# The order of the products with the high and the low part of the weights inside one unit of a panel

## The chip, the cores and the metric

The kernel runs on one core of one Trainium2 chip. The metric is the time of one execution on the device in microseconds (us); of the kernel before there are three runs, and their median counts. One more execution was recorded by the profiler; all rows of the trace come from that one.

## The reference

A decoder trunk of two layers over 256 tokens with a model width of 2048, in 32-bit floats. What matters here is that nearly all of its work is products of a matrix of activations (256 tokens x 2048) with matrices of weights:

```
z = h @ w_in                                   # layer 0: gated linear attention, layer 1: forgetting attention
x = x + concatenate([o, m]) @ w_out            # o: the mixer's heads, m: four heads that attend to 256 memory tokens
u = causal_dwconv(h @ w_up, conv_w, conv_b)    # the channel mixer, 2048 -> 2 x 5632, depthwise convolution of width 3
a, val = split_cols(u, [FFN_HIDDEN, FFN_HIDDEN])
x = x + (silu(a) * val) @ w_down               # 5632 -> 2048
```

h is x after an RMS norm. Between the two layers keys, values and forget gates of the second layer are computed from x in the same way.

## The kernel before, in words

**Two parts of each number.** TensorE multiplies numbers of the type fp32r. Each activation and each weight is split into a high part, rounded to that type, and a low part, the rest. A product is then three products: high with high, high with low and low with high. An activation chunk is a tile `[128, 2, 256]` (bufA and bufB, sixteen each): 128 features on the partitions, then the high part of 256 tokens and behind it the low part.

**Panels and units.** The weights are repacked on the host into panels (`_panels`, `_layout`), in the order of use. A panel's weights come in units of up to 1024 columns of 128 rows, 512 KB, and each unit has one load. There are two kinds of panels:

- 122 panels with *features on the partitions* (`fm`, multiplied by `proj_fm`, L213): 256 output features, 16 chunks of 128 input features, four units of four chunks. They make the keys, queries and gates, and the up-projection of both channel mixers (88 of the 122).
- 42 panels with *tokens on the partitions* (`tm`, `proj_tm`, L248): values, the output projections and the down-projections. There the activations are the stationary operand, and each chunk has three products, high x high at L272, the weights' low part at L273, and the activations' low part at L274. In a panel 512 columns wide each of them has 512 moving columns. The change doesn't touch them.

**A unit of proj_fm.** `split_unit` (L204) loads a unit (`raw`, four buffers, queue of SyncE, L198 and L200), casts it to the high part on ScalarE (`whi`, three buffers, L201), and subtracts on VectorE for the low part (`wlo`, three buffers, L210). Then for each of its four chunks j and each half c of the 256 output features `product` (L232) is called. The weights are the stationary operand, 128x128, loaded into TensorE for each product. With the high part of the weights the moving operand is the whole chunk, 512 columns (the high part of the tokens, then their low part, L235); with the low part it is the chunk's high part alone, 256 columns (L236). Both add to the accumulator of c, a PSUM tile of 512 columns (`acc`, four buffers, two to a panel). So a unit has eight products with the high part and eight with the low part, taken in turn. In a panel's last chunk the low part comes first, and the high part ends the accumulation (L238).

**After a panel.** `evac` of each half: ScalarE copies the second 256 columns out (`whole`, L243), VectorE adds the first 256 (L245), and what follows depends on the panel. In the channel mixer that is the convolution, the activation, and the split of the result into the next chunk (L306, L310).

**What sets the order.** The code's order is a wish: a planner simulates the engines and gives each of them a fixed list of instructions. It takes them by priority, which is the place in the code, and where one isn't ready by its own estimates of time it takes a later one first. Instructions on one accumulator keep their order. `tc.high_priority(offset=AHEAD)` around `split_unit` pulls loads, casts and subtractions 300 places ahead. On the chip each engine works off its list in order and waits on semaphores.

**Start of a stage.** The sixteen chunks for a panel come from the stage before: transposes of the stream on TensorE (L842), then the split into two parts on ScalarE and VectorE (L309, L310). Chunks 12 to 15 come last.

Of the kernel before, what the change touches and what calls it, by code (L numbers as in the profile page):

```python
# [19 lines left out]
P = 128  # L20
T = 256
# [117 lines left out]
def _trunk(ctx: ExitStack, tc: tile.TileContext, xt, xtok, memt, wp, wgu, gns, gfin, cnv, par, msk, out):  # L139
    nc = tc.nc  # L140
    where, _ = _layout()
    V, S, TE = nc.vector, nc.scalar, nc.tensor
# [8 lines left out]
    part = const.tile([P, C_N], F32, name="part")  # L151
# [52 lines left out]
    def split_unit(unit, pieces=1, before=None, pool=wpool, whole=False):  # L204
        with tc.high_priority(offset=AHEAD):
            raw, hi, w = load_unit(unit, pieces, before, pool, whole)
            lo = pool.tile([P, NUNIT], F32R, name="wlo", tag="wlo", bufs=3)
            for i in range(pieces):
                s = slice(i * w // pieces, (i + 1) * w // pieces)
                V.tensor_tensor(lo[:, s], raw[:, s], hi[:, s].bitcast(F32), ALU.subtract)  # L210
        return hi, lo

    def proj_fm(key, src, evac, before=None):  # L213

        units = where[key]
        total = sum(len(u[1]) for u in units)
        acc = [pacc.tile([P, 512], F32, name="acc", tag="acc") for _ in range(2)]
        base = min(min(u[1]) for u in units)
        done = 0
        for n, unit in enumerate(units):  # L220
            if before is None:
                hi, lo = split_unit(unit)
            else:
                hi, lo = split_unit(unit, 2, lambda half: before(n, half), whole=n > 0)
            for j, kc in enumerate(unit[1]):
                for c in range(2):
                    product(acc[c], c, total - 1, done, src[kc - base], hi, lo, j)
                done += 1
        for c in range(2):
            evac(c, acc[c])  # L230

    def product(a, c, last, done, both, hi, lo, j):  # L232
        s = slice(j * 256 + c * P, j * 256 + (c + 1) * P)
        if done < last:
            TE.matmul(a, hi[:, s], both, start=done == 0, stop=False)  # L235
        TE.matmul(a[:, :T], lo[:, s], both[:, 0, :], start=False, stop=False)  # L236
        if done == last:
            TE.matmul(a, hi[:, s], both, start=False, stop=True)  # L238

    def whole(a):  # L240

# [185 lines left out]
    with tc.tile_pool(name="load", bufs=1) as lp:  # L427
# [38 lines left out]
        def first_out(c, a):  # L466
            mk_out(0, 0)(c, a)
            if c == 1:
# [9 lines left out]
                nrm.acc = acc[:, 0, :]  # L478

        proj_fm(("mk", 0, 0), bufA, first_out, before=take_mem)  # L480
        proj_fm(("mk", 0, 1), bufA, mk_out(0, 1))
        xf = [lp.tile([P, T], F32, name=f"xf{i}") for i in range(KC)]
        with tc.issue_after(loads[-1].ins):
# [7 lines left out]
        for j in range(2):  # L491
            proj_fm(("mk", 1, j), bufA, mk_out(1, j))
            if j == 0:
                with tc.issue_after(loads[-1].ins):
                    for f in range(4):
                        nc.sync.dma_start(x[f], xtok[f])
                for f in range(4):
                    for b in range(2):
                        nx.add(f, b)
# [329 lines left out]
    def preparing(name, dst, also=None):  # L829
        n = StreamNorm()  # L830

        def then(f, b):
            n.add(f, b)
            if b == 0:
                return
            for i in range(4 * f, 4 * f + 4, 2):
                ps = work("s", 2)
                for j in range(2):
                    for c in range(2):
                        o = j * T + c * P  # L840
                        k = (i + j) % 4 * P
                        TE.transpose(ps[:, o : o + P], x[f][:, c, k : k + P], ident)  # L842
                for j in range(2):
                    split(dst, i + j, ps[:, j * T : (j + 1) * T], gain(name, i + j))
                if also is not None:
                    also(i, ps)

        return n, then

    gla(nx)  # L850
    n, then = preparing("ffn0", bufB)
# [14 lines left out]
    n, then = preparing("ffn1", bufA)  # L866
# [118 lines left out]
```

## Time and profile before

| | |
|---|---|
| median of 3 runs | 2298.16 us (2298.02 to 2298.43) |
| the profiled execution's own time | 2298.03 us |
| its span, first to last instruction | 2296.2 us |
| TensorE products / weight loads | 12384 / 12384 |
| DVE (VectorE) / ACT (ScalarE) busy | 1619.1 us / 1253.6 us |
| moved from and to memory | 430.15 MB, 187 GB/s in the mean |

How to read it: PE is TensorE's matmuls, PEld its weight loads, which overlap them. DVE is VectorE, ACT ScalarE, SP SyncE; L235 is line 235 of the kernel. In a row of a group, `acc<-B,whi` is the output tile and its inputs, then come partitions and columns, count, busy us, the mean ns of one, and the idle time of the engine ahead of them with what ended it. A row of the timeline begins with the start and the length in us, and ends with how many like instructions in a row it merges. A matmul's end in the records is modelled, and records of matmuls overlap: the distance from start to start is the pace, not the length.

### The profile page before, as it was taken

Reading aid. Unit: us, or ns where it says so; the run is one execution under the profiler, and the core shown is the slowest. Engines: PE = TensorE matmul, PEld = TensorE weight load, DVE = VectorE, ACT = ScalarE, POOL = GpSimd, SP = SyncE. Lnnn points to the kernel's source line nnn. Section 1 sums busy time; section 2 is a strip of 40 time slices with the busy share of each in tenths; the row PEclk is TensorE's granted clock in tenths of the full one; section 3 lists DMA queues with packets and bytes.
Section 4 is the critical chain, followed back from the end, with each engine's and each line's share of the span. In section 5 each row is a group of like instructions: output and inputs, shape, how many; then the busy total and the mean of one; then the engine's idle time right before and its main releaser. Section 6 shows DMA issues by size and latency. Waiting matters only on the chain.

```text
span 2296.2 us, 33165 instructions
## 1 busy us (share of the span) xinstructions
PE 2284.1 (99%) x12384; PEld 1976.2 (86%) x12384; DVE 1619.1 (71%) x2667; ACT 1253.6 (55%) x1967; POOL 3.1 (0%) x20
## 2 busy tenths in 40 slices
PE   9999999999999999999999999999999999999998
PEld 7889888888888888888888998888888888888886
DVE  7578987577765777557767557657776577756775
ACT  7555555555553555445565455556554455534554
POOL 0000000000000000000000000000000000000000
PEclk9999999999999999999999999999999999999999
DMA  8655455555555555555555664555555555665554
GB/s 320 196 162 161 156 164 179 187 184 189 190 189 194 188 191 187 193 192 191 186 183 187 182 194 152 170 193 184 188 189 192 192 191 186 191 193 192 185 192 156
DMA packets 124745, 430.15 MB, mean 187 GB/s; under 512 B 14108, under 2 KB 18600, under 8 KB 124456
## 3 DMA queue, kind: packets, MB, share of 16 engines
q1 hardware_dynamic: 124152, 427.24, 57.3%
q8 instruction: 97, 1.59, 0.3%
q10 hardware_dynamic: 432, 0.79, 0.1%
q14 instruction: 64, 0.52, 0.1%
HBM read 425.87 MB, written 2.11 MB: 186 GB/s over the span
## 4 chain that ended last, share of the span: by engine, by line
PE 99%; DMA 0%; DVE 0%; ACT 0%; issue 0%; DVEq 0%; ACTq 0%; SPq 0%
PE acc L235 37%; PE acc L236 20%; PE acc L273 12%; PE acc L274 12%; PE acc L272 12%; PE acc L238 2%; PE ps_s L842 0%; PE ps_s L631 0%; PE ps_t L402 0%; PE ps_s L409 0%; PE ps_o L420 0%; PE ps_s L756 0%; PE ps_o L772 0%; PE ps_o L650 0%; DMA raw<-wp 0%; DMA cb<-cdram 0%
## 5 line engine op out<-in xcount | busy, mean ns | idle before, releaser
L210 DVE TENSOR_TENSOR wlo<-raw,whi 128x1024 fp32r<-128x1024 f32 (+4 forms) x812 | 972.8, 1199 | 542.3 <-ACT whi L201 531.3
L201 ACT ACTIVATE whi<-raw 128x1024 fp32r<-128x1024 f32 (+4 forms) x812 | 843.5, 1040 | 778.4 <-PE acc L274 373.7
L235 PE MATMUL acc<-B,whi 128*128 128x512 f32 x1980 | 683.6, 395 | 0.0
L235 PE MATMUL acc<-A,whi 128*128 128x512 f32 x1680 | 580.9, 397 | 1.3 <-DVE A L310 1.3
L236 PE MATMUL acc<-B,wlo 128*128 128x256 f32 x2112 | 550.0, 281 | 0.0
L236 PE MATMUL acc<-A,wlo 128*128 128x256 f32 x1792 | 464.0, 281 | 0.0
L235 PEld LDWEIGHTS acc<-B,whi 128*128 128x128 f32 x1980 | 360.7, 188 | 68.5
L236 PEld LDWEIGHTS acc<-B,wlo 128*128 128x128 f32 x2112 | 397.4, 188 | 21.9
L235 PEld LDWEIGHTS acc<-A,whi 128*128 128x128 f32 x1680 | 305.7, 188 | 58.7 <-DVE A L310 2.0
L236 PEld LDWEIGHTS acc<-A,wlo 128*128 128x128 f32 x1792 | 338.3, 189 | 20.2
L273 PE MATMUL acc<-wlo,B 128*128 128x512 f32 (+3 forms) x736 | 274.8, 374 | 0.9 <-DVE wlo L210 0.9
L274 PE MATMUL acc<-whi,B 128*128 128x512 f32 (+3 forms) x736 | 273.6, 372 | 0.0
L272 PE MATMUL acc<-whi,B 128*128 128x512 f32 (+3 forms) x736 | 247.2, 372 | 0.0
L273 PE MATMUL acc<-wlo,A 128*128 128x512 f32 x544 | 212.3, 390 | 0.0
L274 PE MATMUL acc<-whi,A 128*128 128x512 f32 x544 | 211.8, 389 | 0.0
L272 PE MATMUL acc<-whi,A 128*128 128x512 f32 x544 | 192.4, 390 | 0.0
L243 ACT ACTIVATE part<-acc 128x256 f32<-128x256 f32 x240 | 89.9, 375 | 156.7 <-PE acc L238 156.6
L273 PEld LDWEIGHTS acc<-wlo,B 128*128 128x128 f32 x736 | 138.2, 188 | 20.5 <-DVE wlo L210 1.2
L274 PEld LDWEIGHTS acc<-whi,B 128*128 128x128 f32 x736 | 138.2, 188 | 18.6
L272 PEld LDWEIGHTS acc<-whi,B 128*128 128x128 f32 x736 | 137.3, 188 | 18.7
L245 DVE TENSOR_TENSOR wholes<-acc,part 128x256 f32<-128x256 f32 x240 | 101.2, 422 | 64.2 <-ACT part L243 63.9
L274 PEld LDWEIGHTS acc<-whi,A 128*128 128x128 f32 x544 | 102.2, 188 | 21.1
(213 smaller groups left out, 1578.5 us busy)
## 6 DMA issues: line engine op xcount, KB each, us to landing
raw<-wp SPq DMA_DIRECT2D x743, 512.0 KB, 3.4
raw<-wp SPq DMA_DIRECT2D x32, 384.0 KB, 3.1
raw<-wp SPq DMA_DIRECT2D x24, 388.0 KB, 3.1
raw<-wp SPq DMA_DIRECT2D x8, 400.0 KB, 3.1
xf<-xt SPq DMA_DIRECT2D x16, 128.0 KB, 4.4
x<-xtok SPq DMA_DIRECT2D x4, 512.0 KB, 7.5
mt<-memt SPq DMA_DIRECT2D x3, 512.0 KB, 6.8
cb<-cdram SPq DMA_DIRECT2D x12, 128.0 KB, 3.2
```

What stands on the lines that cost most here:

```text
L201: casts.append(S.activation(hi[:, s], raw[:, s], AF.Copy))
L210: V.tensor_tensor(lo[:, s], raw[:, s], hi[:, s].bitcast(F32), ALU.subtract)
L235: TE.matmul(a, hi[:, s], both, start=done == 0, stop=False)
L236: TE.matmul(a[:, :T], lo[:, s], both[:, 0, :], start=False, stop=False)
L238: TE.matmul(a, hi[:, s], both, start=False, stop=True)
L243: S.activation(t, a[:, T:], AF.Copy)
L245: V.tensor_tensor(r, a[:, :T], t, ALU.add)
L272: TE.matmul(a, xk[:, 0, xs], hi[:, s], start=u == 0 and j == 0, stop=False)
L273: TE.matmul(a, xk[:, 0, xs], lo[:, s], start=False, stop=False)
L274: TE.matmul(a, xk[:, 1, xs], hi[:, s], start=False, stop=last)
```

## The change

`product` goes, and its work moves into `proj_fm`. A unit's eight steps (chunk j, half c) are listed once. Then all eight products with the weights' high part come, then all eight with the low part. In the last unit of a panel it is the other way round: the low part's eight first, then the high part's eight, of which the last two chunk products, one for each half, end the accumulation. Operands, sizes, accumulators and the number of instructions stay.

```diff
         units = where[key]
-        total = sum(len(u[1]) for u in units)
         acc = [pacc.tile([P, 512], F32, name="acc", tag="acc") for _ in range(2)]
         base = min(min(u[1]) for u in units)
-        done = 0
         for n, unit in enumerate(units):
             if before is None:
                 hi, lo = split_unit(unit)
             else:
                 hi, lo = split_unit(unit, 2, lambda half: before(n, half), whole=n > 0)
-            for j, kc in enumerate(unit[1]):
-                for c in range(2):
-                    product(acc[c], c, total - 1, done, src[kc - base], hi, lo, j)
-                done += 1
+            steps = [(c, j, src[kc - base]) for j, kc in enumerate(unit[1]) for c in range(2)]
+            ends = n == len(units) - 1
+            for part in ((1, 0) if ends else (0, 1)):
+                for c, j, both in steps:
+                    s = slice(j * 256 + c * P, j * 256 + (c + 1) * P)
+                    if part:
+                        TE.matmul(acc[c][:, :T], lo[:, s], both[:, 0, :], start=False, stop=False)
+                    else:
+                        TE.matmul(acc[c], hi[:, s], both, start=n == 0 and j == 0,
+                                  stop=ends and j == len(unit[1]) - 1)
         for c in range(2):
             evac(c, acc[c])
-
-    def product(a, c, last, done, both, hi, lo, j):
-        s = slice(j * 256 + c * P, j * 256 + (c + 1) * P)
-        if done < last:
-            TE.matmul(a, hi[:, s], both, start=done == 0, stop=False)
-        TE.matmul(a[:, :T], lo[:, s], both[:, 0, :], start=False, stop=False)
-        if done == last:
-            TE.matmul(a, hi[:, s], both, start=False, stop=True)
```

## Prediction

> **What bounds the kernel now.** I read the page from the top: the engines' shares, the granted clock, the chain that ended last; then the groups of instructions.
>
> ```profile
> span 2296.2 us, 33165 instructions
> PE 2284.1 (99%) x12384; PEld 1976.2 (86%) x12384; DVE 1619.1 (71%) x2667; ACT 1253.6 (55%) x1967; POOL 3.1 (0%) x20
> PEclk9999999999999999999999999999999999999999
> PE acc L235 37%; PE acc L236 20%; PE acc L273 12%; PE acc L274 12%; PE acc L272 12%; PE acc L238 2%; PE ps_s L842 0%; PE ps_s L631 0%; PE ps_t L402 0%; PE ps_s L409 0%; PE ps_o L420 0%; PE ps_s L756 0%; PE ps_o L772 0%; PE ps_o L650 0%; DMA raw<-wp 0%; DMA cb<-cdram 0%
> ...
> L235 PE MATMUL acc<-B,whi 128*128 128x512 f32 x1980 | 683.6, 395 | 0.0
> L235 PE MATMUL acc<-A,whi 128*128 128x512 f32 x1680 | 580.9, 397 | 1.3 <-DVE A L310 1.3
> L236 PE MATMUL acc<-B,wlo 128*128 128x256 f32 x2112 | 550.0, 281 | 0.0
> L236 PE MATMUL acc<-A,wlo 128*128 128x256 f32 x1792 | 464.0, 281 | 0.0
> L273 PE MATMUL acc<-wlo,B 128*128 128x512 f32 (+3 forms) x736 | 274.8, 374 | 0.9 <-DVE wlo L210 0.9
> ```
>
> TensorE is the bound: 99% of the span, and 59% of the chain on the three lines that the change rewrites (L235, L236, L238). Its idle time before those lines is 1.3 us in all, before L273 0.9 us, so nothing is to be won from waits on data. The clock stands at 9 in all forty slices, so that won't move either. What can move is the rhythm: how far one product starts after the one before. A record's length doesn't tell that (395 ns for a product with the high part, "hi" from here; 281 ns for one with the low part, "lo"), since records overlap. I count products in stretches that hold one kind only: the first stretch below holds nothing but panels with features on the partitions, the second nothing but proj_tm, where each product is 512 columns wide and never a lo of 256.
>
> ```profile
> core 0: us, PE busy (x) PEld busy (x) DVE busy (x) ACT busy (x) POOL busy (x), PEclk, DMA share, GB/s
> 742.00:920.00 178.00, 178.00 (x1022) 155.40 (x1021) 138.14 (x216) 102.56 (x154) 0.00 (x0) 1.00 0.58 189
> 655.00:741.00 86.00, 86.00 (x381) 71.20 (x380) 46.15 (x48) 35.90 (x37) 0.00 (x0) 1.00 0.59 194
> ```
>
> Each product has one weight load. 178.00 us / 1021 = 174.3 ns a product, or **348.7 ns for a pair** of hi and lo. In the other stretch 86.00 / 380 = **226.3 ns** a product of 512 columns. Next I looked at the pairs one by one, in the timeline of TensorE.
>
> ```profile
> 602.37 0.40 PE L235 MATMUL acc<-B,whi 128*128 128x512 f32 x1
> ...
> 604.11 0.39 PE L235 MATMUL acc<-B,whi 128*128 128x512 f32 x1
> 604.34 0.27 PE L236 MATMUL acc<-B,wlo 128*128 128x256 f32 x1
> 604.45 0.62 PE L235 MATMUL acc<-B,whi 128*128 128x512 f32 x2
> 604.91 0.40 PE L236 MATMUL acc<-B,wlo 128*128 128x256 f32 x2
> 605.15 0.40 PE L235 MATMUL acc<-B,whi 128*128 128x512 f32 x1
> ...
> 606.92 0.40 PE L235 MATMUL acc<-B,whi 128*128 128x512 f32 x1
> ```
>
> Two things are to be seen. At a unit's start (604.45) the planner already put two hi in a row and then two lo, since it took the low part to be late: the order in the code is not wholly the order on the engine. And the alternation has two rhythms without any wait: 602.37 to 604.11 is five pairs, 348 ns each; 605.15 to 606.92 is five pairs too, 354 ns each. Same shapes, same buffers' kinds, next unit.
>
> **The change, part by part.** *What stays.* The products are the same: 1980 + 1680 + 132 + 112 = 3904 hi and 2112 + 1792 = 3904 lo, in 122 panels of 32 pairs (four units of eight). Loads of weights, casts, subtractions, evacuations and DMAs are untouched in number. So the sum is the rhythm in the new order, plus what waits may arise.
>
> *Rhythm inside a row.* A row of hi has the sizes of proj_tm's products, 512 moving columns and a fresh 128x128 load each, so 226.3 ns from the stretch above. A row of lo has 256 columns; no long one exists. proj_tm with 384 columns gives the slope:
>
> ```profile
> 203.69 0.33 PE L273 MATMUL acc<-wlo,B 128*128 128x384 f32 x1
> ...
> 204.73 0.33 PE L272 MATMUL acc<-whi,B 128*128 128x384 f32 x1
> ```
>
> Six products lie between these starts: 1.04 / 6 = 173.3 ns. So 128 columns cost 226.3 - 173.3 = 53.0 ns, and 256 columns 173.3 - 53.0 = 120.3 ns. My estimate for a pair in rows is 226.3 + 120.3 = **346.6 ns**, 2.1 ns under the 348.7 of now. It is also, within rounding, the better of the two rhythms above: the alternation pays no more than two products by themselves, except in the units that fall into the 354 ns rhythm. Longer rows of one shape stay in one rhythm throughout proj_tm, which is why I take the lower figure.
>
> *Ends of rows.* The trace shows what a switch costs.
>
> ```profile
> 18.50 0.52 PE L236 MATMUL acc<-A,wlo 128*128 128x256 f32 x3
> 18.85 0.40 PE L238 MATMUL acc<-A,whi 128*128 128x512 f32 x1
> ...
> 654.72 0.63 PE L272 MATMUL acc<-whi,A 128*128 128x512 f32 x2
> 655.19 0.39 PE L273 MATMUL acc<-wlo,A 128*128 128x512 f32 x1
> ```
>
> After alternating pairs the first two 512-wide products take 0.47 us, 17 ns more than 2 x 226.3. Three lo in a row take 0.35 us, 11 ns less than 3 x 120.3. So a row of hi and the row of lo behind it pay about 17 - 11 = 6 ns at their ends. The last unit goes lo first, and so its eight lo join those of the third unit and its eight hi those of the next panel's first: three such pairs of ends a panel, not four, 18 ns.
>
> *Sum.* Now: 32 x 348.7 = 11158 ns a panel. After: 32 x 346.6 + 18 = 11109 ns. Saved: 49 ns x 122 panels = **6.0 us**. From the profiled execution's 2298.03 us (span 2296.2 and 1.8 around it) that is 2292.0; the median of the runs is 0.13 above it, so 2292.2 us.
>
> *Bounds of the unknown row.* For a row of lo the nearest rows are the three at 18.50 (117 ns each, a short row's gain kept) and the slow rhythm's pair (354 - 226.3 = 128 ns). The first gives 3904 x (120.3 - 117) = 13 us less than my sum, the second 30 us more. I take 120.3, which lies nearest to proj_tm, the only long rows there are.
>
> *Weight loads under a row of lo.* [...]
>
> ```profile
> 599.82 0.28 PE L236 MATMUL acc<-B,wlo 128*128 128x256 f32 x1
> 599.82 0.19 PEld L235 LDWEIGHTS acc<-B,whi 128*128 128x128 f32 x1
> 599.93 0.39 PE L235 MATMUL acc<-B,whi 128*128 128x512 f32 x1
> 599.94 0.19 PEld L236 LDWEIGHTS acc<-B,wlo 128*128 128x128 f32 x1
> ```
>
> Today each lo hides the load of a hi and starts its successor 0.11 to 0.12 us later; in a row it hides the load of a lo, of the same 128x128 shape. So one short slot covers one load either way, and I cost it at nothing. But the cover is thin: a load's record is 0.19 us, and today a long hi slot follows each short one, in which the loads can catch up. In a row of eight or sixteen lo they can't. If that matters, each lo is later by what the load lacks.
>
> The Trainium skill, "TensorE: Matmul & The Clock Gate", section "LDWEIGHTS (loading the stationary operand)", puts a load at its columns / 1.2 ns, 107 ns for 128, and by its section "Back-to-back issue gap" 256 columns stream in 109 ns. By these two a row of lo is as much bound by loads as by streaming, with 2 ns to spare, where a hi leaves over 100; it speaks against the new order wherever a load has any cost beyond its columns. The trace's 120.3 ns a lo would leave 13 ns for that.
>
> *Waits on the low part.* In units one to three lo starts after eight hi instead of after one or two: looser. In the last unit it is needed at the unit's start, 0.46 us earlier than now (604.45 to 604.91). The supply:
>
> ```profile
> 601.79 1.06 ACT L201 ACTIVATE whi<-raw 128x1024 fp32r<-128x1024 f32 x1 [0.84 <-ACT cv L816]
> 602.89 1.23 DVE L210 TENSOR_TENSOR wlo<-raw,whi 128x1024 fp32r<-128x1024 f32 x1
> ```
>
> Of three buffers the cast fills the one that the unit ending at 601.67 gave back; it is used two units later, at about 601.67 + 2 x 2.79 = 607.25, and is full at 604.12. Three us of slack cover the 0.46. Without that cover it would be 0.46 x 122 = 56 us. The high part comes back to ACT after eight products instead of at the unit's end, so casts start earlier, and the transfers into raw behind them no later. The accumulators' evacuation has a whole panel, 11 us, since two other accumulators are in use meanwhile.
>
> *Sources at the start of a stage.* With lo first, the last unit needs its fourth chunk after six lo, 0.7 us in, rather than 2.1 us in. The tightest such place is the first up panel:
>
> ```profile
> 481.58 0.48 DVE L310 SCALAR_TENSOR_TENSOR B<-ps_s,gains,B 128x256 fp32r<-128x256 f32 x1
> ...
> 484.07 0.40 PE L235 MATMUL acc<-B,whi 128*128 128x512 f32 x1
> ```
>
> The last chunk is there at 482.06, and the fourth unit starts at 484.07 (eight hi a unit, counted from 474.75): 2.0 us of slack, so nothing.
>
> **The rivals.** *No change.* The rhythm keeps its mix whatever the order, because two hi and two lo at 604.45 to 605.15 took 0.70 us, 350 ns a pair, no better than alternation; or the planner interleaves the rows again as it does at 604.45, and the change doesn't do what it says. For it: that row. Against it: proj_tm's steady rows. 2298 us.
>
> *Slower, rows of lo bound by their loads.* The place is each row of eight or sixteen lo. The price is that of the slow rhythm, 354 ns a pair: 3904 x (354 - 348.7) = 21 us, 2319 us. It decides from (6.0 + 4.6) / 3904 = 2.7 ns a lo on: then the time is 0.2% over now. For it: 0.19 us loads in 0.12 us slots. Against: the three lo at 18.50 show no growth.
>
> *Slower, waits.* The planner may put lo of the last unit, or small products of the attention, where the in-order engine meets data that isn't there; 0.46 us once a panel is the 56 us above, 2354 us. Against: three us of slack.
>
> **How the numbers follow.** Forecast (rows in proj_tm's rhythm) 0.44, no change 0.30, bound by loads 0.20, waits 0.06. A measurement of this kernel can tell about 0.2%, 4.6 us. So faster 0.44, same 0.30, slower 0.26. The range goes down to 2286, half of the way to the bound by three-lo rows, and up to 2319, the slow rhythm; it leaves out the waits and lesser tails.
>
> **What would show it.** Right: in 178 us of panels alone about 1025 loads (64 x 178.00 / 11.109) instead of 1021; timelines with eight hi at 0.226 us spacing and lo at 0.12; idle before L235's and L236's successors still near zero. Wrong: lo spaced over 0.123 us while loads stand back to back (loads bind); rows broken up (planner); an idle column with "DVE wlo L210" behind it (waits). The forecast fails if hi in a row keep 0.23 us or more.

## The result and the profile after

The changed kernel takes **2294.75 us** in the median of 21 runs (2294.08 to 2295.21); the kernel before, measured beside it, 2298.10 us (2297.98 to 2298.73). The ratio is 0.9985, with a 95% interval of 0.9979 to 0.9991: 3.35 us or 0.15% less, which is clear of the noise. The forecast was 2292.2 us, 6.0 less. The prediction had drawn the line between "faster" and "the same" at 4.6 us; by that line the result is "the same", to which it gave 0.30, so the time alone says little about the mechanism, and the starts of the products have to.

These lines of the page of the changed kernel answer to those of before. L233 is now every product with the weights' high part (hi), L231 every one with the low part (lo), and L270 to L272 are proj_tm. An up panel is one of the 88 panels of the up-projections.

```profile
span 2293.2 us, 33186 instructions
PE 2280.3 (99%) x12384; PEld 1985.1 (87%) x12384; DVE 1606.3 (70%) x2667; ACT 1243.3 (54%) x1967; POOL 3.1 (0%) x20
...
L233 PE MATMUL acc<-B,whi 128*128 128x512 f32 x2112 | 524.2, 393 | 0.0
L233 PE MATMUL acc<-A,whi 128*128 128x512 f32 x1792 | 445.7, 394 | 1.1 <-DVE A L308 1.1
...
L231 PE MATMUL acc<-B,wlo 128*128 128x256 f32 x2112 | 289.4, 283 | 0.0
L271 PE MATMUL acc<-wlo,B 128*128 128x512 f32 (+3 forms) x736 | 275.1, 374 | 1.9 <-DVE wlo L210 1.9
...
L231 PE MATMUL acc<-A,wlo 128*128 128x256 f32 x1792 | 245.8, 284 | 0.0
```

TensorE is the bound as before, and the products with the low part wait for nothing: 0.0 on both L231 rows. The busy times of L231 fell from 1014 us to 535 us, and that means nothing: busy time is a union, and records of lo that follow each other overlap more than alternating ones. The mean lengths are nearly the same (283 against 281 ns). The pace has to be read from starts. This is the timeline of TensorE in a stretch with nothing but up panels; each row is one row of like products.

```profile
749.93 3.82 PE L233 MATMUL acc<-B,whi 128*128 128x512 f32 x16
753.59 1.12 PE L231 MATMUL acc<-B,wlo 128*128 128x256 f32 x8
754.54 2.00 PE L233 MATMUL acc<-B,whi 128*128 128x512 f32 x8
756.38 1.11 PE L231 MATMUL acc<-B,wlo 128*128 128x256 f32 x8
757.34 2.00 PE L233 MATMUL acc<-B,whi 128*128 128x512 f32 x8
759.18 2.08 PE L231 MATMUL acc<-B,wlo 128*128 128x256 f32 x16
761.09 3.82 PE L233 MATMUL acc<-B,whi 128*128 128x512 f32 x16
...
783.39 3.82 PE L233 MATMUL acc<-B,whi 128*128 128x512 f32 x16
```

The order is what the code says: rows of 8 and 16, unbroken here. From 749.93 to 783.39 are three panels, **11.153 us** each. In the kernel before, two panels lie between these two rows:

```profile
763.96 0.39 PE L238 MATMUL acc<-B,whi 128*128 128x512 f32 x1
...
786.29 0.39 PE L238 MATMUL acc<-B,whi 128*128 128x512 f32 x1
```

22.33 / 2 = 11.165 us; over all up panels the starts give 11.169. So an up panel gained 16 ns, not 49.

Taken start by start, the rows show why. Every row of hi ends at 226.7 ns a product and every row of lo runs at 120.0. But the first five hi behind a row of lo start 233.3, 235.8, 228.3, 232.5 and 230.8 ns apart, 27 ns more in all than five of 226.7; the first two lo behind a row of hi take 113.4 and 119.2, 7.5 ns less than two of 120.0. The up panels that nothing cuts all take the same time, within 1 ns. A way from hi to lo and back costs **20 ns**, and a panel has three of them: 32 x 346.7 + 60 = 11153.

The two profiled spans differ by 3.0 us, and the 88 up panels account for 16 x 88 = 1.4 of it. By the starts of the panels, 0.2 us comes before the first panel, 0.6 and 0.35 us in the two stretches that hold the other 34 panels, and the remaining 0.5 us lies around the down-projections between the up panels. Against it stands 1.0 us more of waiting on wlo ahead of L271, 0.9 us before and 1.9 now. The 34 panels are cut up by small products, and I have no finer account of them. Over the whole execution the spacings behind hi sum to 901.8 us instead of 914.2, those behind lo to 470.0 instead of 460.5: the hi won 12.4 us and the lo lost 9.5.

### The profile page after: what moved, and what is told of

The parts are those of the page before. It is cut to its first block, busy times and chain, and to the rows that moved or that the text cites. A ratio compares the mean times of both kernels' runs of the same rounds, so it can differ in the third digit from the quotient of the medians.

```text
span 2293.2 us, 33186 instructions
## 1 busy us (share of the span) xinstructions
PE 2280.3 (99%) x12384; PEld 1985.1 (87%) x12384; DVE 1606.3 (70%) x2667; ACT 1243.3 (54%) x1967; POOL 3.1 (0%) x20
## 4 chain that ended last, share of the span: by engine, by line
PE 98%; DVE 1%; DMA 0%; issue 0%; ACT 0%; DVEq 0%; ACTq 0%; SPq 0%
PE acc L233 39%; PE acc L231 20%; PE acc L271 12%; PE acc L272 12%; PE acc L270 12%; PE ps_s L840 0%; PE ps_s L629 0%; PE ps_t L400 0%; PE ps_s L407 0%; PE ps_o L418 0%; PE ps_s L754 0%; PE ps_o L770 0%; PE ps_o L648 0%; DMA raw<-wp 0%; DMA cb<-cdram 0%
## 5 line engine op out<-in xcount | busy, mean ns | idle before, releaser
L233 PE MATMUL acc<-B,whi 128*128 128x512 f32 x2112 | 524.2, 393 | 0.0
L233 PE MATMUL acc<-A,whi 128*128 128x512 f32 x1792 | 445.7, 394 | 1.1 <-DVE A L308 1.1
L233 PEld LDWEIGHTS acc<-B,whi 128*128 128x128 f32 x2112 | 382.7, 189 | 70.7
L233 PEld LDWEIGHTS acc<-A,whi 128*128 128x128 f32 x1792 | 326.4, 189 | 62.0 <-DVE A L308 1.9
L231 PEld LDWEIGHTS acc<-B,wlo 128*128 128x128 f32 x2112 | 281.2, 191 | 16.3
L231 PE MATMUL acc<-B,wlo 128*128 128x256 f32 x2112 | 289.4, 283 | 0.0
L271 PE MATMUL acc<-wlo,B 128*128 128x512 f32 (+3 forms) x736 | 275.1, 374 | 1.9 <-DVE wlo L210 1.9
L272 PE MATMUL acc<-whi,B 128*128 128x512 f32 (+3 forms) x736 | 273.1, 371 | 0.0
L231 PEld LDWEIGHTS acc<-A,wlo 128*128 128x128 f32 x1792 | 239.0, 191 | 13.5
L270 PE MATMUL acc<-whi,B 128*128 128x512 f32 (+3 forms) x736 | 247.9, 372 | 0.0
L231 PE MATMUL acc<-A,wlo 128*128 128x256 f32 x1792 | 245.8, 284 | 0.0
L271 PE MATMUL acc<-wlo,A 128*128 128x512 f32 x544 | 212.3, 390 | 0.0
L272 PE MATMUL acc<-whi,A 128*128 128x512 f32 x544 | 211.7, 389 | 0.0
L270 PE MATMUL acc<-whi,A 128*128 128x512 f32 x544 | 192.7, 390 | 0.0
L271 PEld LDWEIGHTS acc<-wlo,B 128*128 128x128 f32 x736 | 138.2, 188 | 21.7 <-DVE wlo L210 2.4
L272 PEld LDWEIGHTS acc<-whi,B 128*128 128x128 f32 x736 | 138.2, 188 | 18.6
L270 PEld LDWEIGHTS acc<-whi,B 128*128 128x128 f32 x736 | 137.3, 188 | 18.8
L814 ACT ACTIVATE cv<-u,cw 128x256 f32<-128x256 f32 x176 | 104.9, 597 | 43.3 <-DVE u L810 43.3
```

Source lines behind the costliest of these rows:

```text
L231: TE.matmul(acc[c][:, :T], lo[:, s], both[:, 0, :], start=False, stop=False)
L233: TE.matmul(acc[c], hi[:, s], both, start=n == 0 and j == 0, stop=ends and j == len(unit[1]) - 1)
L270: TE.matmul(a, xk[:, 0, xs], hi[:, s], start=u == 0 and j == 0, stop=False)
L271: TE.matmul(a, xk[:, 0, xs], lo[:, s], start=False, stop=False)
L272: TE.matmul(a, xk[:, 1, xs], hi[:, s], start=False, stop=last)
L814: S.activation(r, u[:, 2:], AF.Identity, bias=w[3], scale=w[2])
```

## The experiments

One theory stood at the start, with three rivals. *Ends theory*: a row has a fixed pace, and each way from lo to hi costs. The rivals: the low part is needed later (waits), the accumulators taking turns cost, or the gain grows in proportion to the rows' length. Before's median beside these runs was 2298.2 to 2298.4 us.

**1. More rows of sixteen.**

```diff
-            for part in ((1, 0) if ends else (0, 1)):
+            for part in ((1, 0) if n % 2 else (0, 1)):
```

> Every second unit takes its low part first, so that rows of sixteen alternate: two changes from lo to hi a panel instead of the changed kernel's three. Ends theory (a row runs at 226.7 and 120.0 ns a product; a change from lo to hi costs 27 ns, the one back gives 7): 20 ns x 122 panels = 2.4 us less than the changed kernel, 2292.3 us. Rival, the gain of the change came from the low part being needed later, so that needing it first in two units of four instead of one costs: 2294.8 us or more, with idle time ahead of L230's and L232's products.

Measured 2293.38 us, ratio to before 0.9978 (0.9969 to 0.9987). One panel in the timeline:

```profile
760.98 3.82 PE L233 MATMUL acc<-B,whi 128*128 128x512 f32 x16
764.63 2.08 PE L231 MATMUL acc<-B,wlo 128*128 128x256 f32 x16
766.54 3.82 PE L233 MATMUL acc<-B,whi 128*128 128x512 f32 x16
770.20 2.08 PE L231 MATMUL acc<-B,wlo 128*128 128x256 f32 x16
772.11 3.82 PE L233 MATMUL acc<-B,whi 128*128 128x512 f32 x16
```

The starts of all up panels give 11.133 us each, 20 ns less than the changed kernel, as the ends theory has it: 1.8 us in 88 panels. The medians differ by 1.4 us, the two profiled spans by 1.9, so the other stages gained next to nothing. No product of a panel waits for its low part, so the rival falls.

**2. Rows of four.** The same loop over half a unit at a time, the last half of a panel turned.

```diff
-            for part in ((1, 0) if ends else (0, 1)):
-                for c, j, both in steps:
+            for g in (0, 2):
+                last = ends and g == 2
+                for part in ((1, 0) if last else (0, 1)):
+                    for c, j, both in steps[2 * g : 2 * g + 4]:
```

> Rows of four hi and four lo (seven changes from lo to hi a panel). Ends theory: the first four hi after lo are 23 ns late in all in the changed kernel's trace, lo give 7 to 8 back, so 16 ns x 7 = 110 ns a panel against 3 x 20 = 60 there: 50 ns x 122 = 6.1 us more than the changed kernel, 2300.9 us, slower than the kernel before although its products are grouped. Rival, grouping helps in proportion to the rows' length: between the two kernels, 2295 to 2298 us.

Measured 2303.07 us, ratio 1.0020 (1.0012 to 1.0029): slower than before, as the ends theory said and its rival did not. The price was 60 ns a panel above the changed kernel's, not 50 (11.213 us a panel), and the stages with small products lost as well. **Grouping is no gain by itself.** Four hi in a row are all among the late first five.

**3. Strict alternation.** The kernel before, with each product of a panel chained behind the one before it in the planner.

```diff
+    fm = []
+
+    def kept(m):
+        if fm:
+            tc.add_manual_dep(m.ins, fm[-1].ins.name, ..., reason="order")
+        fm.append(m)
...
-            TE.matmul(a, hi[:, s], both, start=done == 0, stop=False)
+            kept(TE.matmul(a, hi[:, s], both, start=done == 0, stop=False))
```

> The kernel before with its products held in the order of the code: hi and lo alternate without the planner's pairs at the start of a unit. Theory that the slow rhythm (353 ns a pair) is set off by those pairs: nearly all pairs run at 347 ns, (349.0 - 347.0) x 3904 = 7.8 us less than before, 2290.3 us, better than the changed kernel. Rival, the two rhythms come with alternation itself: 2298 us, or up to 2314 us if the slow one spreads.

Measured 2309.73 us, ratio 1.0049 (1.0037 to 1.0062): the rival was right and my theory wrong. The pairs that the planner had made did not set off the slow rhythm, they mostly *broke* it. In the up panels of the kernel before the alternation behind such a pair runs at 347 ns in most units, and at 353 as a rule in a panel's third unit. Without the pairs it runs at 353 ns a pair nearly from a panel's first product to its last:

```profile
777.82 0.40 PE L247 MATMUL acc<-B,whi 128*128 128x512 f32 x1
...
789.12 0.40 PE L247 MATMUL acc<-B,whi 128*128 128x512 f32 x1
```

11.30 us a panel, 131 ns more than before. So the kernel before owed its pace in part to a planner's estimate that happened to break the alternation once a unit. The rows of four of experiment 2, slower than the kernel before, are 6.7 us faster than strict alternation.

**4. Fewer changes of accumulator.**

```diff
-            steps = [(c, j, src[kc - base]) for j, kc in enumerate(unit[1]) for c in range(2)]
+            steps = [(c, j, src[kc - base]) for c in range(2) for j, kc in enumerate(unit[1])]
```

> The changed kernel with the four products of one accumulator in a row inside each row of eight: the accumulator changes twice a row instead of eight times. Ends theory: same changes between hi and lo, same time, 2294.8 us within 0.5. Rival, taking turns between two accumulators costs part of the 27 ns at a row's start or of the spacing: at least 1 us off.

Measured 2295.07 us, ratio 0.9986 (0.9977 to 0.9995): no difference. The accumulators' turns cost nothing.

**5. Rows of 32.** In the up panels two units are worked off together, the second two from buffers of their own (`more`: the pool of the stage in layer 0, the pool of the end in layer 1).

```diff
-                hi, lo = split_unit(unit)
+                hi, lo = split_unit(unit, pool=more if more is not None and n > 1 else wpool)
...
+            if more is not None and n % 2 == 0:
+                continue
```

> The first experiment's order (turned in every second unit), and in the 88 up panels two units together: sixteen hi, sixteen lo, then lo and hi of the other two, so rows of 32 and one change from lo to hi a panel. The second pair of units has buffers of its own there. Ends theory: 20 ns x 88 = 1.8 us less than the first experiment, 2291.6 us, below both kernels. Rival, a long row of lo runs out of low parts, since VectorE has to have four ready: waits on wlo, 2293.4 us or more.

Measured 2298.87 us, ratio 1.0002 (0.9993 to 1.0011): a miss, 7 us off, and not by the rival's cause, since no lo of a panel waited. The panels of layer 1 show where the time goes:

```profile
1840.43 7.56 PE L235 MATMUL acc<-A,whi 128*128 128x512 f32 x32
1847.82 3.99 PE L233 MATMUL acc<-A,wlo 128*128 128x256 f32 x32
1851.65 7.56 PE L235 MATMUL acc<-A,whi 128*128 128x512 f32 x32
```

7.39 us for 32 hi are 231 ns each. Start by start, the hi from the first buffers come down to 226.7, those from the second buffers don't: in layer 1 they repeat 230.8, 231.9, 237.2 (233.3 in the mean), in layer 0 they stand at 232.5 in the mean. The lo from the second buffers, with 256 columns, are no slower than 120 ns in the mean. The tiles' addresses in the built program differ: the first buffers begin 256 bytes behind a multiple of 512, the second ones 128 behind in layer 0 and 160 in layer 1. That made a new theory, *place*, for experiments 9 to 11.

**6. Without the turned last unit.**

```diff
-            for part in ((1, 0) if ends else (0, 1)):
+            for part in (0, 1):
```

> The changed kernel without its turned last unit: eight hi, then eight lo in each unit, four changes from lo to hi a panel instead of three, and the last lo of each half ends the accumulation. Ends theory: 20 ns x 88 to 122 = 1.8 to 2.4 us more than the changed kernel, 2296.5 to 2297.2 us. Rival, the turn was worth nothing by itself or cost waits: 2294.8 us or less.

Measured 2296.61 us, ratio 0.9992 (0.9983 to 1.0001), 1.9 us above the changed kernel, and 11.173 us an up panel, 20 ns more: the fourth way back costs what the third did. With one to four ways in an up panel (experiments 9 and 1, the changed kernel, experiment 6) the times are 2290.76, 2293.38, 2294.75 and 2296.61 us.

**7 and 8. Is it the weight loads?** 384 moving columns in each product with the low part, in the changed kernel (7) and in strict alternation (8), leave each load 53 ns more cover.

```diff
-                        TE.matmul(acc[c][:, :T], lo[:, s], both[:, 0, :], start=False, stop=False)
+                        TE.matmul(acc[c][:, :384], lo[:, s], both.rearrange("p a t -> p (a t)")[:, :384], start=False, stop=False)
```

> The changed kernel with 384 moving columns instead of 256 in each product with the low part (the low part of half the tokens is multiplied too), so that a lo lasts longer than a weight load. Cover theory (the ends cost because a row of 256-column lo leaves no room for its loads): lo at 173.3 ns, hi at 226.7 ns from the first one behind a row of lo on, a panel of 12.80 us, 2294.8 + 122 x (12.800 - 11.153) = 2495.7 us. Rival, the switch of sizes itself costs: hi again at 233, 236, 228, 232, 231 ns behind a row of lo, some 2503 us.

> Strict alternation as in the third experiment, with 384 moving columns in each product with the low part. Cover theory: pairs at 226.7 + 173.3 = 400.0 ns, no slow rhythm, 2496 us, the same as the seventh experiment within 3 us. Rival, alternation of two sizes has a slow rhythm whatever the sizes: 406 ns a pair or more, 2515 us or more.

Measured 2517.69 and 2543.92 us, one run each: the first is above even its rival's figure, the second is where its rival had put it, "2515 us or more". The cover theory falls with both. In experiment 7:

```profile
850.20 2.01 PE L233 MATMUL acc<-B,whi 128*128 128x512 f32 x8
852.05 2.96 PE L231 MATMUL acc<-B,wlo 128*128 128x384 f32 x16
...
863.20 2.01 PE L233 MATMUL acc<-B,whi 128*128 128x512 f32 x8
```

From the first row to the last is one panel, 13.00 us instead of the 12.80 of the cover theory. The eight hi behind a row of these wider lo take 1.85 us, 231 ns each; in rows of sixteen they settle at 226.7 from the tenth on. And the way from hi to lo, which gave 7.5 ns back with 256 columns, now costs 28 to 30 ns: the wider lo reach 173.3 ns only after six. In alternation a pair took 413 ns instead of 400 (a panel of 13.227 us / 32):

```profile
850.08 0.40 PE L244 MATMUL acc<-B,whi 128*128 128x512 f32 x1
...
851.74 0.40 PE L244 MATMUL acc<-B,whi 128*128 128x512 f32 x1
```

Four pairs lie between these two, 1.66 us to the hundredth. More room under the short product makes the change of size no cheaper, here even dearer.

**12. One size.** Strict alternation once more, each product with the low part over all 512 columns.

```diff
-        TE.matmul(a[:, :T], lo[:, s], both[:, 0, :], start=False, stop=False)
+        kept(TE.matmul(a, lo[:, s], both, start=False, stop=False))
```

> Strict alternation as in the third experiment, but each product with the low part has 512 moving columns too (it multiplies the tokens' low part as well), so all products are of one size. Size theory (a change of size throws the pace off, and alternation changes it at each product): all at 226.7 ns, pairs of 453.3 ns in spite of the alternation of buffers, and no first slow products. Rival, alternation of the two weight buffers or accumulators costs by itself: over 460 ns a pair.

Measured 2706.69 us, in one run. All products of the up panels start 226.7 ns apart, from the first to the last, a panel in 14.507 us = 64 x 226.7:

```profile
993.08 0.39 PE L244 MATMUL acc<-B,whi 128*128 128x512 f32 x1
...
1007.58 0.39 PE L244 MATMUL acc<-B,whi 128*128 128x512 f32 x1
```

Alternating buffers, accumulators and loads cost nothing; what costs comes with **the change of size**, that of the moving operand and so of the columns added to. It doesn't cost every time: in the kernel before, stretches of alternation at 347 ns a pair pay no more than the two paces by themselves. What decides between 347 and 353 is not shown.

**9. Rows of 32 from buffers in line.** Experiment 5 with two unused tiles that move the second buffers to 256 bytes behind a multiple of 512.

```diff
+            if spare is None:
+                pad = fp.tile([P, 32], F32, name="pad")
...
+        pad = op.tile([P, 24], F32, name="pad")
```

> The fifth experiment with an unused tile of 128 bytes a partition (layer 0) and of 96 (layer 1) ahead of the second buffers, so that all weight buffers begin 256 bytes behind a multiple of 512, as the first ones do. Place theory (the products from the second buffers ran off the rhythm, hi at 232.5 to 233.3 ns, because of where these begin): hi at 226.7 and lo at 120.0 ns there too, 2291.6 us. Rival, rows of 32 or the longer wait for buffers slow it: 2298.9 us again.

Measured **2290.76 us**, ratio 0.9967 (0.9955 to 0.9980): the fastest kernel here, 4.0 us below the changed one, in spite of one wait of 0.9 us of a lo for its low part.

```profile
780.76 7.44 PE L235 MATMUL acc<-B,whi 128*128 128x512 f32 x32
788.04 4.00 PE L233 MATMUL acc<-B,wlo 128*128 128x256 f32 x32
791.87 7.44 PE L235 MATMUL acc<-B,whi 128*128 128x512 f32 x32
...
802.98 7.44 PE L235 MATMUL acc<-B,whi 128*128 128x512 f32 x32
```

22.22 / 2 = 11.11 us a panel, 32 x 346.7 + 20 = 11114. Only the tiles' places differ from experiment 5, so they were the cause of the 8 us between the two.

**10. Everything 256 bytes on.**

```diff
+    pad = const.tile([P, 64], F32, name="pad")
     x = [const.tile([P, 2, 512], F32, name=f"x{f}") for f in range(4)]
```

> The changed kernel with an unused tile of 256 bytes a partition ahead of the stream, so that activations and weights all begin at a multiple of 512 bytes instead of 256 behind one. Place theory leaves two ways: if what counts is a grid of 256 bytes, nothing changes, 2294.8 us within 1; if it is one of 512 bytes, the spacing of 226.7 ns moves, either way, by 2 ns or more a product, 15 us or more. Rival, place has no effect: 2294.8 us.

Measured 2294.68 us, ratio 0.9984 (0.9975 to 0.9994): no change. Both multiples of 256 serve alike.

**11. The weight buffers, and what is allocated behind them, 128 bytes on.**

```diff
     mv = [const.tile([P, 2, MEM_H * HD], F32, name=f"mv{l}") for l in range(2)]
+    pad = const.tile([P, 32], F32, name="pad")
```

> The changed kernel with an unused tile of 128 bytes a partition ahead of the weight buffers alone: they begin 384 bytes behind a multiple of 512, the activations stay. Place theory: hi in rows at about 232.5 ns as from the fifth experiment's second buffers in layer 0, 3904 x 5.8 = 23 us more, 2317 us; up to 2340 us if the products of proj_tm, where the weights are the moving operand, lose as much. Rival, place has no effect: 2294.8 us.

Measured 2322.26 us, ratio 1.0104 (1.0090 to 1.0118). A panel and proj_tm in its timeline and its windows, the latter beside a window of the changed kernel:

```profile
803.19 3.88 PE L235 MATMUL acc<-B,whi 128*128 128x512 f32 x16
...
814.42 3.88 PE L235 MATMUL acc<-B,whi 128*128 128x512 f32 x16
```

```profile
660.00:745.00 85.00, 85.00 (x368) 68.91 (x367) 44.71 (x47) 34.73 (x37) 0.00 (x0) 1.00 0.58 187
```

```profile
655.00:740.00 85.00, 85.00 (x377) 70.38 (x376) 45.40 (x46) 34.77 (x36) 0.00 (x0) 1.00 0.59 191
```

A panel takes 11.23 us instead of 11.153, and proj_tm's products 85.00 / 367 = 231.6 ns instead of 85.00 / 376 = 226.1; by their starts, without the products that a window's edge cuts, 232.4 instead of 226.7. So both uses of the weights lose, as the moving and as the stationary operand, at the same granted clock of 1.00. The pad moves not only the weights, as the expectation has it, but every tile allocated behind them too; the chunks of activations stay. The starts settle what counts: over the whole execution the distances behind hi sum to 12.0 us more than in the changed kernel and those behind proj_tm's products to 18.2 more, those behind lo to 2.4 less, and those behind all other products change by 0.3. So the expected 2317 us came near for the wrong reason: it put 23 us on hi, which cost half of that, and left proj_tm, the larger part, to its upper figure. And products of 256 columns don't lose at all.

## Why the prediction was right or wrong

The direction and the mechanism, a steadier pace in rows, were right. The size was not, and the sum came as near as it did in part by luck, since three terms that were off partly cancel.

*What bounds the kernel*: right. The engine, its clock and its idle time stayed, and the rhythm moved.

*Rhythm inside a row*: right. 226.3 and 120.3 ns were worked out from proj_tm's rows of 512 and 384 columns; 226.7 and 120.0 came.

*The pace now*: too short. 348.7 ns a pair, 11158 ns a panel, came from a count of products in a window of 178 us, where a product or two cut by the window's ends is 0.1 to 0.2%. The starts give 11169 ns. Those 11 ns a panel are a fifth of the gain forecast. The sign that I named, the count of loads in a window, has the same weakness: in 742 to 918 us, panels alone in both kernels, it is 1014 against 1009, five more, where 16 ns a panel make one or two. A window that doesn't end where a panel ends holds more of the short products or fewer.

*Ends of rows*: **here the sum failed by size.** I took 6 ns for a row of hi and the row of lo behind it; it is 20. I had read the surcharge of hi from two products, 17 ns, and stopped there. In rows behind lo it lasts five, 27 ns, and the very row that I read was late for longer than two; the same trace has

```profile
654.49 0.39 PE L238 MATMUL acc<-B,whi 128*128 128x512 f32 x1
...
656.11 0.40 PE L274 MATMUL acc<-whi,A 128*128 128x512 f32 x1
```

with seven products of 512 columns between these starts, 1.62 us or 231 ns each. And the gain of lo, 11 ns from three in a row, is 7.5; the timeline rounds to 10 ns. With 60 ns of ends a panel instead of 18 the sum gives 7 ns, not 49. With the pace now set right as well it gives 16, as the starts do, and times 122 a forecast of about 2296.2 us. The measured gain, 3.35 us, lies between these 2.0 us and the 6.0. What is beyond the 2.0 comes from outside the up panels, and the prediction had no term for it.

*The slow rhythm of 354 ns*: I took it for a state into which some units fall. Experiment 3 shows that it is the state of alternation here, and that the kernel before was kept out of it, in most units, by the pairs of its planner.

*Weight loads under a row of lo*: costed at nothing, and rightly. These two rows of the changed kernel are a row of sixteen lo and its loads, cut at 748.70:

```profile
748.02 0.88 PE L231 MATMUL acc<-B,wlo 128*128 128x256 f32 x6
748.03 0.78 PEld L231 LDWEIGHTS acc<-B,wlo 128*128 128x128 f32 x6
```

Each load begins just behind the start of the product ahead of it, and the spacing stays at 120.0 ns to the last of the sixteen; in experiment 9 to the last of thirty-two. The rival at 2319 us has fallen. What spoke for it, a load's record of 0.19 us, is no time that a product waits for: in the lines of before the load at 599.82 ends at 600.01 by its record, and its product starts at 599.93. The Trainium skill, "TensorE: Matmul & The Clock Gate", "LDWEIGHTS (loading the stationary operand)", gives 107 ns a load. Loads and products 120 ns apart fit that, but no record here shows the 107 ns itself.

*Waits on the low part, sources at a stage's start*: right. No product of a panel waited for a low part, and the one wait on a chunk (1.1 us, 1.3 before) was there already. The unexpected wait is proj_tm's, 1.9 us instead of 0.9, a thousandth of the span at most.

*The rival of no change*: its time of 2298 us was too long, but its row, 0.70 us for two hi and two lo, was the better witness for what an end costs: 350 ns a pair against the 346.7 of rows.

*The order on the engine*: the planner kept the rows in the up panels, so there the change does what it says.

## What to carry to other kernels

A stream of products that keeps TensorE busy has a pace, and it is read from the distance of starts, not from busy time or mean length. Where sizes are mixed, count how often the size changes and look for how many products the pace takes to settle, before you price a reordering; rows shorter than that can be slower than the order that they replace, as experiment 2 shows. And when tiles move, compare their addresses: a pad of 96 or 128 bytes was worth more here than the change under study.

## What the runs showed of the hardware that I had not expected

- A change of size between rows of eight or more products costs 20 ns there and back (512 and 256 columns); the pace settles over five products. With 512 and 384 columns it takes nine, and the way from long to short costs too.
- Strict alternation of 512 and 256 columns runs at 353 ns a pair, 6.5 ns more than the sum of the two paces; of 512 and 384, at 413, 13 ns more than 400. Broken by a pair once a unit, the alternation of 512 and 256 runs at 347 in most units. Alternating products of one size keep 226.7 ns.
- Weights that begin off a multiple of 256 bytes slow the products of 512 columns that read them: at 128 bytes off 232.4 instead of 226.7 ns in proj_tm, 27.5 us in the kernel. Products of 256 columns with such weights as the stationary operand keep 120 ns. A shift of weights and activations by 256 bytes changes nothing.
- The pace of 226.7 ns for 512 columns differs from the Trainium skill, "TensorE: Matmul & The Clock Gate", section "Back-to-back issue gap". It gives 512 / 2.4 + 2.5 = 216 ns for the gap of a product taken by itself and about 131 ns a product for a stream of loads and products at 512 columns. No run here shows either; the measurement decides.

What inside the engine loses the pace at a change of size, and why a grid of 256 bytes matters, stays open: the runs show that each costs time, and how much.
